# Seven-product weight chunks: one weight sum made by an adding transfer, and the sums and products in another order

## The chip, the cores and the metric

One Trainium2 chip; the kernel runs on one of its cores. The metric is the device time of one execution in microseconds (us). The engines are TensorE (PE in the profile; its weight loads are PEld), VectorE (DVE), ScalarE (ACT), GpSimd (POOL) and SyncE (SP, which here only starts transfers).

## The reference, cut to what matters

A model of two layers on 256 tokens of width 1024, all in fp32. Each layer has a first feed-forward block, a token mixer, a cross attention and a second feed-forward block, each followed by a layer norm:

```python
def swiglu(x, w_gate, w_up, w_down):
    return (jax.nn.silu(x @ w_gate) * (x @ w_up)) @ w_down

for l in range(2):
    h = layer_norm(ALPHA * h + 0.5 * swiglu(h, ffn1_gate[l], ffn1_up[l], ffn1_down[l]), ln_g[l, 0], ln_b[l, 0])
    ...
    h = layer_norm(ALPHA * h + 0.5 * swiglu(h, ffn2_gate[l], ffn2_up[l], ffn2_down[l]), ln_g[l, 3], ln_b[l, 3])
```

The gate and up weights are 1024 x 2816, the down weight is 2816 x 1024. There are four such blocks in all; the change is in them alone.

## The kernel before, in words

**Products.** An fp32 product is made of three matmuls. Every 128 x 1024 piece of a weight is loaded to a `raw` tile; ACT copies it, rounded, to a high part `whi`, and DVE subtracts that from the raw values to make the low part `wlo` (`split`, L60; ACT is L61, DVE is L62). The activations have the same two parts (`xTh` and `xTl`, `ah` and `al`). `mm_rows` (L129) then issues, for each slice of 128 rows, high x high, high x low and low x high, so the second matmul of every three is the first that reads `wlo`. There are 8 `whi` and 8 `wlo` buffers, given out in turn.

**The feed-forward block** is `ffn` (L400). The 2816 columns are cut into six chunks, five of 512 and one of 256. For a chunk the kernel makes gate and up products, then SiLU(gate) x up (`sg`); four transfers and two transposes on DVE turn that around (`turn`, L446), and it is split into `ah` and `al`. The products with the down weight (`both`, L683, accumulated in the PSUM tiles `dn`) follow one chunk behind: after the hidden products of chunk c come the second half of chunk c-2's down products and the first half of chunk c-1's, each half being one call of `both` with 24 matmuls.

**Chunks of seven products.** The chunks in `sevens` (L666) are computed by a block scheme with seven products of half the size instead of eight: chunks 2 and 4 of each block, and in the first block of layer 0 (the one with `early`) only chunk 4. That makes seven such chunks in all. The tokens, the 1024 rows of the weights and the pair (gate, up) are each halved. `w00` is gate rows 0 to 511, `w10` gate rows 512 to 1023, `w01` up rows 0 to 511, `w11` up rows 512 to 1023, each 512 columns wide and held in two tiles of 128 x 1024. `bx[0]` to `bx[3]` are four combinations of the activations that `blocks_of_x` (L539) makes once for a block. Each product is one call of `run` (L597): four slices of three matmuls, so 12 matmuls, 84 for a chunk.

`by_seven` (L555) issues the loads, then goes through the products in this order, making the parts of each product's weight just ahead of it (`parts_of`, L580; with a second argument it first adds that block into the first, in place, two adds of 128 x 1024 on DVE, L584). PSUM results are combined into `g[0]`, `g[1]`, `e` and `f` by DVE (`put`, L605 and L606) and one ACT copy (L612):

| product | weight | adds of 128 x 1024 ahead of it |
|---|---|---|
| 1 | w00 | none |
| 2 | w00 += w01 | 2 |
| 3 | w00 += w11 | 2 |
| 4 | w01 += w11 | 2 |
| 5 | w11 | none |
| 6 | w10 | none |
| 7 | w00 += w10 | 2 |

The last combinations are in `left` (L628), which runs after `both(c - 2, 1)`.

**What orders the work.** Each engine works through its instructions in one order, set ahead by a scheduler from the program and its buffers. `w00` lies in the tiles `spare0` and `spare1`, `w01` in `lng` and `lnb` (these hold the layer norm's parameters at other times: `ln_params`, L293, loads them for the block's end at chunk 5), `w11` and half of `w10` in the rotating `raw` tiles, the other half of `w10` in `spare2`. All weight loads are issued by SP.

Of the kernel before, what the change touches and what calls it, by code (L numbers as in the profile page):

```python
# [46 lines left out]
def model(ctx: ExitStack, tc: tile.TileContext, t: dict, out: bass.AP):  # L47
# [352 lines left out]
    def ffn(l, name, n, pend=None, last=False, early=None):  # L400
        gate, up, down = (t[f"{name}_{x}"][l] for x in ("gate", "up", "down"))
        with tc.tile_pool(name="ffn", bufs=2, reuse_waits="tile") as fp:
# [40 lines left out]

            def turn(s):  # L446
                ah, al = act_tiles()
                x = fp.tile([P, 4, NT, P], F32, tag="dealt", name="dealt", bufs=1)
                for a in range(4):
                    nc.sync.dma_start(x[a * 32 : a * 32 + 32], s[:, :, a * P : (a + 1) * P])  # L450
                for i in range(NT):
                    d = fp.tile([P, 4, P], F32, tag="up", name="square")
                    nc.vector.transpose(
                        d.rearrange("p k (b r) -> p b k r", b=4), x[:, :, i, :].rearrange("p b (k j) -> p b k j", k=4)
                    )
                    split(ah[:, :, tok(i)], al[:, :, tok(i)], d)
                return ah, al

            def first():
# [62 lines left out]
                        gated(s, i, ou)  # L522
                return turn(s)

            def hidden(c0, between=lambda: None):
                s = activations()
                o = all_products(load(gate, 0, NK, c0, CHUNK))
                for i in range(NT):
                    activate(s, i, o[i])
                between()  # L530
                o = all_products(load(up, 0, NK, c0, CHUNK))
                for i in range(NT):
                    gated(s, i, o[i])
                return turn(s)
# [17 lines left out]
                    split(*parts[n], q[o])  # L552
                return parts

            def by_seven(c0, bx):  # L555
                def rows_by_columns(r):
                    return r.rearrange("p (k c) -> p k c", c=CHUNK)

                def pieces(*tags):
                    return [  # L560
                        rows_by_columns(
                            (fp if "spare" in g else wp).tile([P, DM], F32, tag=g, name="raw", bufs=6 if g == "raw" else 1)
                        )
                        for g in tags
                    ]

                def block(m, j, to):
                    for i in range(2):
                        k = 4 * j + 2 * i
                        loads.append(nc.sync.dma_start(  # L570
                            to[i], m[k * P : (k + 2) * P, c0 : c0 + CHUNK].rearrange("(k p) c -> p k c", p=P)
                        ))
                    return to
# [6 lines left out]
                def parts_of(r, plus=None):  # L580
                    hi, lo = [], []
                    for i in range(2):
                        if plus is not None:
                            nc.vector.tensor_tensor(r[i], r[i], plus[i], op=ALU.add)  # L584
                        h = wp.tile([P, 1024], F32R, tag="whi", name="whi", bufs=8)
                        w = wp.tile([P, 1024], F32R, tag="wlo", name="wlo", bufs=8)
                        h, w = (rows_by_columns(x) for x in (h, w))
                        split(h, w, r[i])
                        hi.append(h)
                        lo.append(w)  # L590
                    return Weights(hi, lo, 2, [])

                def part_of_x(i, j):
                    d = slice(4 * j, 4 * j + 4)
                    return xTh[:, d, tok(i)], xTl[:, d, tok(i)]

                def run(o, x, w):  # L597
                    for k in range(4):
                        wh, wl = w.at(k, slice(0, CHUNK))
                        mm_rows(o, x[0][:, k, :], x[1][:, k, :], wh, wl, k == 0, k == 3)  # L600

                def half_sum():
                    return fp.tile([P, 4, P], F32, tag="up", name="half").rearrange("p k t -> p (k t)")

                def put(o, a, op, b):  # L605
                    nc.vector.tensor_tensor(halves(o), sums(a), halves(b), op=op)  # L606

                s = activations()
                g = [s[:, i, :] for i in range(NT)]
                o = [acc((P, CHUNK)) for _ in range(4)]  # L610
                run(o[0], part_of_x(0, 0), parts_of(w00))
                nc.scalar.copy(halves(g[0]), sums(o[0]))  # L612
# [12 lines left out]
                run(o[2], part_of_x(1, 1), parts_of(w00, w10))  # L625


                def left():  # L628
                    put(e, o[0], ALU.add, e)
                    for i in range(NT):  # L630
                        put(g[i], o[1 + i], ALU.add, g[i])
                    s = fp.tile([P, NT, CHUNK], F32, tag="spare2", name="sg", bufs=1)
                    for i, u in enumerate((e, f)):
# [3 lines left out]
                    return turn(s)  # L637

                return left

# [50 lines left out]
            def aside():  # L691

                with tc.issue_after(lows[-1].ins):
                    if bx:
                        rest[1]()
                    else:
                        bx.extend(blocks_of_x())

            for c, (c0, ncol) in enumerate(chunks):
                if not c:  # L700
                    acts.append(first())
                    ys = [[acc((P, 512), "dn") for _ in range(2)] for _ in range(NT)]
                elif c in sevens:
                    left = by_seven(c0, bx)
                else:
                    if c in (1, 2) and early is not None:
                        acts.append(hidden(c0, aside))
                    else:
                        acts.append(hidden(c0) if ncol == CHUNK else last_hidden(c0))
                if c == 1 and early is None:  # L710
                    bx.extend(blocks_of_x())
                if c == max(sevens) + 1:
                    gb = ln_params(l, n)
                if c == 1 and early is not None:

# [492 lines left out]
```

## Time and profile before

| quantity | value |
|---|---|
| time, median of 3 runs | 1072.19 us (1072.14 to 1073.27) |
| the profiled execution's own time | 1072.23 us |
| its span in the trace | 1070.2 us, so 2.0 us lie outside the span |
| granted TensorE clock, mean | 0.998 |
| busy: PE, DVE, ACT, POOL | 1060.6, 946.3, 642.2, 65.0 us |
| bytes moved by transfers | 231.90 MB |

The profile is of one execution. Busy time is the time in which an engine had an instruction under way. The chain of waits follows the work that ended last back to its start. Windows give the busy time of each engine in a stretch of the span; a row of the timeline joins neighbouring instructions of one kind (x3 is three of them). A line of the table by line that has one line number for a helper (L62, L105) joins all its callers.

### The profile page before, as it was taken

To read this page: it belongs to the slowest core of one execution; us is meant where nothing else is said; L and a number is where in the kernel's file an instruction comes from. 1 tells how busy PE (TensorE), PEld (TensorE's weight loads), DVE (VectorE), ACT (ScalarE), POOL (GpSimd) and SP (SyncE) were. 2 spreads that over 40 slices of the span, in tenths; PEclk is the share of its full clock that TensorE was granted. 3 is DMA by queue.
4 is the path that set the end of the run, shared out by engine and by line. 5 is a ranking of instruction groups with operands and counts; after the bars stand their busy time and mean duration, and the time that the engine had idled before them with its cause. 6 is when DMAs were issued, how large, how long until landed. Compare 5 with 4: busy or idle time off the path is not lost.

```text
span 1070.2 us, 16314 instructions
## 1 busy us (share of the span) xinstructions
PE 1060.6 (99%) x5968; PEld 938.9 (88%) x5968; DVE 946.3 (88%) x1318; ACT 642.2 (60%) x916; POOL 65.0 (6%) x114
## 2 busy tenths in 40 slices
PE   9999999999999999999999999999999999999997
PEld 7888888889899888888888888888898998888886
DVE  6977997998998799999799999788989787999986
ACT  7556655767457565656575557566764665656660
POOL 9600001000000000000000000010000000000000
PEclk9999999999999999999999999999999999999999
DMA  9998395755575575948675875957536665759471
GB/s 360 259 298 269 119 281 167 251 188 159 177 271 168 181 247 198 292 167 226 236 260 192 250 261 173 298 168 227 190 128 208 247 230 176 259 151 341 133 220 40
DMA packets 130896, 231.90 MB, mean 217 GB/s; under 512 B 9409, under 2 KB 48609, under 8 KB 130817
## 3 DMA queue, kind: packets, MB, share of 16 engines
q1 hardware_dynamic: 129024, 228.49, 65.6%
q0 software_dynamic: 1216, 1.20, 0.5%
q8 instruction: 47, 0.77, 0.3%
q10 hardware_dynamic: 576, 1.18, 0.3%
q14 instruction: 33, 0.26, 0.1%
HBM read 216.15 MB, written 1.05 MB: 203 GB/s over the span
## 4 chain that ended last, share of the span: by engine, by line
PE 99%; DMA 0%; DVE 0%; issue 0%; DVEq 0%
PE acc L105 65%; PE dn L105 31%; PE acc L172 1%; PE dn L910 1%; DMA h<-in_x_dram 0%; PE dn L969 0%; PE dn L968 0%; PE dn L958 0%; PE acc L1034 0%; PE dn L472 0%; PE dn L875 0%; DVE h L358 0%; DVE h L353 0%; DVE st L338 0%; DVE h L326 0%
## 5 line engine op out<-in xcount | busy, mean ns | idle before, releaser
L61 ACT CAST whi<-raw 128x1024 fp32r<-128x1024 f32 (+1 forms) x438 | 442.4, 1042 | 199.3 <-DVE raw L584 54.7
L62 DVE TENSOR_TENSOR wlo<-raw,whi 128x1024 fp32r<-128x1024 f32 (+1 forms) x438 | 515.6, 1210 | 33.9 <-ACT whi L61 30.4
L105 PE MATMUL acc<-whi,xT 128*128 128x512 f32 x1032 | 312.9, 380 | 0.0
L105 PEld LDWEIGHTS acc<-whi,xT 128*128 128x128 f32 x1032 | 195.0, 189 | 27.5
L105 PE MATMUL acc<-wlo,xT 128*128 128x512 f32 x516 | 195.6, 379 | 0.0
L105 PE MATMUL acc<-xT,whi 128*128 128x512 f32 x576 | 142.2, 382 | 0.2
L105 PE MATMUL dn<-whi,ah 128*128 128x512 f32 x346 | 131.5, 380 | 0.0
L105 PE MATMUL dn<-wlo,ah 128*128 128x512 f32 x346 | 131.1, 379 | 0.0
L105 PE MATMUL dn<-whi,al 128*128 128x512 f32 x346 | 131.1, 379 | 0.0
L105 PEld LDWEIGHTS acc<-xT,whi 128*128 128x128 f32 x576 | 103.9, 190 | 12.5 <-ACT whi L61 0.7
L105 PEld LDWEIGHTS acc<-wlo,xT 128*128 128x128 f32 x516 | 97.5, 189 | 13.9
L105 PE MATMUL dn<-whi,xT 128*128 128x512 f32 x288 | 87.9, 381 | 0.0
L105 PEld LDWEIGHTS acc<-xT,wlo 128*128 128x128 f32 x576 | 75.5, 191 | 3.9
L105 PE MATMUL acc<-xT,wlo 128*128 128x256 f32 x576 | 75.9, 275 | 0.0
L105 PEld LDWEIGHTS dn<-wlo,ah 128*128 128x128 f32 x346 | 65.4, 189 | 9.2
L105 PEld LDWEIGHTS dn<-whi,al 128*128 128x128 f32 x346 | 65.4, 189 | 9.2
L105 PEld LDWEIGHTS dn<-whi,ah 128*128 128x128 f32 x346 | 65.4, 189 | 9.1
L584 DVE TENSOR_TENSOR raw<-raw 128x1024 f32<-128x1024 f32 x56 | 66.2, 1218 | 0.4
L350 POOL TENSOR_TENSOR rs<-rs,nhalf 128x1 f32<-128x1 f32 x16 | 14.9, 929 | 834.2 <-DVE rs L346 598.7
L105 PEld LDWEIGHTS dn<-whi,xT 128*128 128x128 f32 x288 | 54.6, 190 | 7.4
L105 PE MATMUL dn<-wlo,xT 128*128 128x512 f32 x144 | 54.6, 379 | 0.0
L332 DVE SCALAR_TENSOR_TENSOR h<-h,dn 128x512 f32<-128x512 f32 x31 | 21.2, 683 | 31.6 <-PE dn L105 31.6
(232 smaller groups left out, 1278.7 us busy)
## 6 DMA issues: line engine op xcount, KB each, us to landing
raw<-in_ffn_up_dram SPq DMA_DIRECT2D x88, 512.0 KB, 5.3
raw<-in_ffn_down_dram SPq DMA_DIRECT2D x88, 512.0 KB, 6.9
raw<-in_ffn_gate_dram SPq DMA_DIRECT2D x84, 512.0 KB, 5.0
raw<-in_w_in_dram SPq DMA_DIRECT2D x48, 512.0 KB, 4.7
dealt<-sg SPq DMA_DIRECT2D x80, 128.0 KB, 4.7
raw<-in_ca_k_dram SPq DMA_DIRECT2D x16, 512.0 KB, 5.1
raw<-in_w_out_dram SPq DMA_DIRECT2D x16, 512.0 KB, 4.3
raw<-in_ca_v_dram SPq DMA_DIRECT2D x16, 512.0 KB, 5.3
```

The source lines that it names most:

```text
L61: nc.scalar.copy(hi, src)
L62: lows.append(nc.vector.tensor_tensor(lo, src, hi.bitcast(F32), op=ALU.subtract))
L105: nc.tensor.matmul(o, w, x, start=start, stop=stop)
L172: nc.tensor.transpose(pt[:, k, :], src[:, (4 * j + k) * P : (4 * j + k + 1) * P], unit)
L332: nc.vector.scalar_tensor_tensor(v, v, ALPHA / scale, sums(y[i][n]), op0=ALU.mult, op1=ALU.add, accum_out=None if junk is None else st[:, ...
L350: nc.gpsimd.tensor_tensor(rs, rs, nhalf[:, 0:1], op=ALU.pow)
L584: nc.vector.tensor_tensor(r[i], r[i], plus[i], op=ALU.add)
L910: nc.tensor.matmul(o[g, hh, :], kc[:, hh, g], x, start=True, stop=True)
```

## The change

The seven products are the same as sets of operands; what makes their weights, and the order, are others.

- The sum `w01 + w11` is called `both_up` and is made by transfers: SP loads `w01` into the tiles `lng` and `lnb` as before (L568 after the change), and GpSimd then starts two transfers of 512 KB that add `w11`'s rows into the same tiles (L578, `accum_op=ALU.add`). That is done in `sum_by_transfers`, from `between()` in the chunk before, that is, between its gate and its up products. `w11` is also loaded by itself, as before.
- DVE's adds of 128 x 1024 (L596 after the change) are three pairs instead of four.
- The order of the products, after:

| product | weight | operations of 128 x 1024 ahead of it |
|---|---|---|
| 1 | w00 | none |
| 2 | w11 | none |
| 3 | w10 | none |
| 4 | w00 += both_up | 2 |
| 5 | both_up | none |
| 6 | both_up = w00 - w11, after product 5's split has read both_up | 2 |
| 7 | w00 += w10, after product 6's subtraction has read w00 | 2 |

- The results of products 1 and 2 are copied from PSUM by ACT (two copies instead of one); DVE still combines seven times (L622 after the change).
- The tiles `lng` and `lnb` are now last read by product 6's splits instead of product 4's, so the load of the layer norm's parameters behind chunk 4 waits for those.
- `turn`, `pieces`, `block` and `by_seven` also take a narrower last chunk; `sevens` does not name one, so that code makes no instructions here. The numbers of matmuls are as before.

The core of the diff:

```diff
+            def sum_by_transfers(c0):
+                to = block(up, 0, c0, pieces("lng", "lnb"))
+                for i, r in enumerate(to):
+                    a = (4 + 2 * i) * P
+                    nc.gpsimd.dma_start(
+                        r, up[a : a + 2 * P, c0 : c0 + CHUNK].rearrange("(k p) c -> p k c", p=P), accum_op=ALU.add
+                    )
+                return to
...
-                w00 = block(gate, 0, pieces("spare0", "spare1"))
-                w01 = block(up, 0, pieces("lng", "lnb"))
-                w11 = block(up, 1, pieces("raw", "raw"))
-                w10 = block(gate, 1, pieces("spare2", "raw"))
+                    w00 = block(gate, 0, c0, pieces("spare0", "spare1"))
+                    w11 = block(up, 1, c0, pieces("raw", "raw"))
+                    w10 = block(gate, 1, c0, pieces("spare2", "raw"))
...
                 run(o[0], part_of_x(0, 0), parts_of(w00))
-                nc.scalar.copy(halves(g[0]), sums(o[0]))
-                run(o[2], bx[0], parts_of(w00, w01))
-                run(o[1], bx[1], parts_of(w00, w11))
                 e = half_sum()
-                put(e, o[1], ALU.add, g[0])
-                run(o[3], bx[2], parts_of(w01, w11))
-                put(g[1], o[3], ALU.add, e)
+                nc.scalar.copy(halves(e), sums(o[0]))
+                run(o[1], bx[3], parts_of(w11))
                 f = half_sum()
-                put(f, o[2], ALU.subtract, g[1])
-                put(e, o[2], ALU.subtract, e)
-                o = [acc((P, CHUNK)) for _ in range(3)]
-                run(o[0], bx[3], parts_of(w11))
-                run(o[1], part_of_x(0, 1), parts_of(w10))
-                run(o[2], part_of_x(1, 1), parts_of(w00, w10))
+                nc.scalar.copy(halves(f), sums(o[1]))
+                run(o[2], part_of_x(0, 1), parts_of(w10))
+                combine(g[0], o[2], ALU.add, e)
+                put(w00, w00, ALU.add, both_up)
+                run(o[3], bx[1], parts_of(w00))
+                combine(e, o[3], ALU.add, e)
+                combine(f, f, ALU.subtract, e, apart=False)
+                o = [acc((P, ncol)) for _ in range(3)]
+                run(o[0], bx[2], parts_of(both_up))
+                combine(g[1], o[0], ALU.add, e)
+                put(both_up, w00, ALU.subtract, w11)
+                run(o[1], bx[0], parts_of(both_up))
+                put(w00, w00, ALU.add, w10)
+                run(o[2], part_of_x(1, 1), parts_of(w00))
...
+                if c + 1 in sevens:
+                    n = (c + 1) * CHUNK
+                    if n + CHUNK <= DFF:
+                        both_up[:] = sum_by_transfers(n)
```

The change moves instructions on DVE. Three places are shown, two of them in chunk 2 of the second feed-forward block of layer 0. Before the change the tiles of w00 are raw_4296 and raw_4297, of w01 raw_4300 and raw_4301, of w11 raw_4304 and raw_4305, of w10 raw_4308 and raw_4309. After it, w00 is raw_4303 and raw_4304, both_up raw_4154 and raw_4155, w11 raw_4307 and raw_4308, w10 raw_4311 and raw_4312.

The first place is DVE from the fifth product's first split to the two splits of the seventh. Before, the fifth product is w11's, and the rows are these:

```order
L62 TENSOR_TENSOR wlo_4414<-raw_4304,whi_4413 128x1024
L62 TENSOR_TENSOR wlo_4418<-raw_4305,whi_4417 128x1024
...
L62 TENSOR_TENSOR wlo_4438<-raw_4309,whi_4437 128x1024
L62 TENSOR_TENSOR wlo_4455<-raw_4296,whi_4454 128x1024
L606 TENSOR_TENSOR sg_4312<-acc_4316,half_4382 128x512
L584 TENSOR_TENSOR raw_4297<-raw_4297,raw_4309 128x1024
L606 TENSOR_TENSOR half_4407<-acc_4315,sg_4312 128x512
L606 TENSOR_TENSOR half_4382<-acc_4315,half_4382 128x512
L62 TENSOR_TENSOR wlo_4460<-raw_4297,whi_4459 128x1024
```

After, the fifth product is both_up's:

```order
L62 TENSOR_TENSOR wlo_4413<-raw_4154,whi_4412 128x1024
L596 TENSOR_TENSOR raw_4154<-raw_4303,raw_4307 128x1024
...
L596 TENSOR_TENSOR raw_4155<-raw_4304,raw_4308 128x1024
L622 TENSOR_TENSOR sg_4315<-acc_4318,half_4340 128x512
L62 TENSOR_TENSOR wlo_4436<-raw_4154,whi_4435 128x1024
...
L596 TENSOR_TENSOR raw_4303<-raw_4303,raw_4311 128x1024
L596 TENSOR_TENSOR raw_4304<-raw_4304,raw_4312 128x1024
L622 TENSOR_TENSOR half_4362<-acc_4410,half_4362 128x512
L62 TENSOR_TENSOR wlo_4458<-raw_4303,whi_4457 128x1024
L62 TENSOR_TENSOR wlo_4462<-raw_4304,whi_4461 128x1024
```

From the fifth product's first split to the seventh's second, counting both, DVE has 7 operations of 128 x 1024 and 8 of 128 x 512 before, and 10 and 9 after: one add of 128 x 1024 (L584) stood between them before, four (L596) do so now.

The second place is DVE just ahead of that, at the splits of the earlier products. Before:

```order
L584 TENSOR_TENSOR raw_4297<-raw_4297,raw_4301 128x1024
L584 TENSOR_TENSOR raw_4296<-raw_4296,raw_4304 128x1024
L584 TENSOR_TENSOR raw_4300<-raw_4300,raw_4304 128x1024
L62 TENSOR_TENSOR wlo_4345<-raw_4297,whi_4344 128x1024
...
L584 TENSOR_TENSOR raw_4297<-raw_4297,raw_4305 128x1024
L584 TENSOR_TENSOR raw_4301<-raw_4301,raw_4305 128x1024
L584 TENSOR_TENSOR raw_4296<-raw_4296,raw_4308 128x1024
L62 TENSOR_TENSOR wlo_4367<-raw_4297,whi_4366 128x1024
```

After:

```order
L596 TENSOR_TENSOR raw_4304<-raw_4304,raw_4155 128x1024
L62 TENSOR_TENSOR wlo_4347<-raw_4308,whi_4346 128x1024
L62 TENSOR_TENSOR wlo_4365<-raw_4311,whi_4364 128x1024
...
L62 TENSOR_TENSOR wlo_4388<-raw_4303,whi_4387 128x1024
L62 TENSOR_TENSOR wlo_4392<-raw_4304,whi_4391 128x1024
L62 TENSOR_TENSOR wlo_4413<-raw_4154,whi_4412 128x1024
```

Six of the eight adds stood here and one ahead; now one stands here and one ahead (`raw_4303<-raw_4303,raw_4154`), and DVE comes to the fifth product's split with five fewer adds behind it.

The third place is in chunk 4 of the same block: DVE from the fourth product's first split to the seventh's first. Before, the fourth product's weight is w01 + w11 (raw_4818 and raw_4819), w00 is raw_4814 and raw_4815:

```order
L62 TENSOR_TENSOR wlo_4904<-raw_4818,whi_4903 128x1024
...
L62 TENSOR_TENSOR wlo_4909<-raw_4819,whi_4908 128x1024
L62 TENSOR_TENSOR wlo_4932<-raw_4822,whi_4931 128x1024
L62 TENSOR_TENSOR wlo_4936<-raw_4823,whi_4935 128x1024
L62 TENSOR_TENSOR wlo_4952<-raw_4826,whi_4951 128x1024
L62 TENSOR_TENSOR wlo_4956<-raw_4827,whi_4955 128x1024
L606 TENSOR_TENSOR half_4900<-acc_4832,sg_4830 128x512
L62 TENSOR_TENSOR wlo_4973<-raw_4814,whi_4972 128x1024
```

After, the fourth product's weight is w00 + both_up (raw_4822 and raw_4823), both_up is raw_4651 and raw_4652:

```order
L62 TENSOR_TENSOR wlo_4907<-raw_4822,whi_4906 128x1024
...
L62 TENSOR_TENSOR wlo_4936<-raw_4652,whi_4935 128x1024
L596 TENSOR_TENSOR raw_4651<-raw_4822,raw_4826 128x1024
L596 TENSOR_TENSOR raw_4652<-raw_4823,raw_4827 128x1024
L622 TENSOR_TENSOR sg_4834<-acc_4837,half_4859 128x512
L62 TENSOR_TENSOR wlo_4955<-raw_4651,whi_4954 128x1024
...
L596 TENSOR_TENSOR raw_4823<-raw_4823,raw_4831 128x1024
L622 TENSOR_TENSOR sg_4834<-acc_4928,half_4859 128x512
L62 TENSOR_TENSOR wlo_4977<-raw_4822,whi_4976 128x1024
```

From the one split to the other, counting both, there were 7 operations of 128 x 1024 and 3 of 128 x 512 (two of these are a transposed chunk's low parts); there are 11 and 6 now, four adds (L596) and three combinations more.

More of the change, by code (lines that the diff above doesn't have):

```diff
@@ L523, in first, with hidden @@
                 return turn(s)
-            def hidden(c0, between=lambda: None):
+            def hidden(c0, between):
                 s = activations()
@@ new lines, in by_seven, with put, parts_of @@
+            def by_seven(c0, bx, both_up=None):
+                ncol = min(CHUNK, DFF - c0)
+                if both_up is not None:
+                    w00 = block(gate, 0, c0, pieces("spare0", "spare1"))
+                    w11 = block(up, 1, c0, pieces("raw", "raw"))
+                    w10 = block(gate, 1, c0, pieces("spare2", "raw"))
+                else:
+                    w00, both_up, w11, w10 = (
+                        block(m, j, c0, pieces("raw", width=ncol)) for m, j in ((gate, 0), (up, 0), (up, 1), (gate, 1))
+                    )
+                def put(o, a, op, b):
+                    for x, y, z in zip(o, a, b):
+                        nc.vector.tensor_tensor(x, y, z, op=op)
+                def parts_of(r):
@@ L608, in by_seven, with combine @@
+                def combine(o, a, op, b, apart=True):
+                    nc.vector.tensor_tensor(halves(o), sums(a) if apart else halves(a), halves(b), op=op)
                 s = activations()
-                g = [s[:, i, :] for i in range(NT)]
-                o = [acc((P, CHUNK)) for _ in range(4)]
+                g = [s[:, i, 0:ncol] for i in range(NT)]
+                if ncol < CHUNK:
+                    put(both_up, both_up, ALU.add, w11)
+                o = [acc((P, ncol)) for _ in range(4)]
@@ L703, in ffn @@
                 elif c in sevens:
-                    left = by_seven(c0, bx)
+                    left = by_seven(c0, bx, both_up if ncol == CHUNK else None)
                 else:
[L706 to L709, printed above, removed]
+                    acts.append(hidden(c0, between) if ncol == CHUNK else last_hidden(c0))
                 if c == 1 and early is None:
                     bx.extend(blocks_of_x())
-                if c == max(sevens) + 1:
+                if c == len(chunks) - 1:
                     gb = ln_params(l, n)
```

87 lines of the change are left out of this document (41 added, 46 removed).

## Prediction

> **What bounds the kernel now.** I read the page first, then the chain of waits, windows over one block's chunks, and the timeline around a chunk of seven products. The page's busy times:
>
> ```profile
> PE 1060.6 (99%) x5968; PEld 938.9 (88%) x5968; DVE 946.3 (88%) x1318; ACT 642.2 (60%) x916; POOL 65.0 (6%) x114
> ```
>
> PE is busy for 1060.6 of 1070.2 us: all that can be gained without fewer matmuls is 9.6 us, and that lies at the ends. The windows (columns: length, then busy time and instructions of PE, PEld, DVE, ACT, POOL, then clock, DMA share, GB/s) show the first 20 us, the stretch ahead of a seven-product chunk 2, that chunk, the same for chunk 4, and the end:
>
> ```profile
> 0.00:20.00 20.00, 17.92 (x76) 14.97 (x77) 13.30 (x18) 13.46 (x19) 19.16 (x41) 1.00 0.92 349
> 396.00:417.00 21.00, 21.00 (x99) 18.39 (x98) 19.95 (x24) 10.65 (x15) 0.00 (x0) 1.00 0.60 207
> 417.00:435.10 18.10, 18.10 (x85) 15.81 (x84) 18.10 (x21) 11.73 (x14) 0.00 (x0) 1.00 0.67 187
> 476.60:494.70 18.10, 18.10 (x85) 15.87 (x84) 18.10 (x21) 14.84 (x16) 0.00 (x0) 1.00 0.55 175
> 1060.00:1080.00 20.00, 2.87 (x26) 2.67 (x24) 5.74 (x14) 0.00 (x0) 0.92 (x1) 0.85 0.13 48
> ```
>
> Inside the chunks PE has no gap, and DVE has none either: it supplies the parts just in time. The chain of waits is PE from end to end (start, length):
>
> ```profile
> 412.00 5.18 PE dn L105 x24
> 417.18 18.13 PE acc L105 x84
> 435.31 10.36 PE dn L105 x48
> ```
>
> So a chunk of seven takes PE 18.13 us, 2.59 us a product, 0.216 us a matmul. PE's own matmuls start at 417.02 (the chain counts 0.16 us later), the fifth product at 427.38, the seventh at 432.56. The question is only whether DVE still delivers each low part by then.
>
> **The adds that go.** The group by line and shape on DVE (busy us, mean ns):
>
> ```profile
> L584 DVE TENSOR_TENSOR raw<-raw 128x1024 f32<-128x1024 f32 x56 | 66.2, 1218 | 0.4
> ```
>
> Two adds fewer in each of seven chunks: 14 x 1.218 = 17.1 us less DVE work. On the path that sets the end it is worth nothing, since PE waits for DVE nowhere in these stages. A rule speaks otherwise: the Trainium skill, Perfetto Trace Analysis, section Identifying the Most-Contended Engine, says to optimize first the engine with the highest occupancy, and to judge TensorE by its weight loads' busy share and not by its matmuls'. By that rule weight loads and DVE stand level (88% each on the page), and DVE's 17.1 us could count in full; the trace disagrees for this kernel, since 84 matmuls fill 18.10 of 18.10 us. I take zero; the most that a gain could be is bounded by the idle 9.6 us, which the change does not touch.
>
> **The adds that move.** DVE's timeline around chunk 2 (start, length, count):
>
> ```profile
> 402.58 1.18 DVE L584 TENSOR_TENSOR raw<-raw 128x1024 f32<-128x1024 f32 x1
> ...
> 407.15 3.49 DVE L584 TENSOR_TENSOR raw<-raw 128x1024 f32<-128x1024 f32 x3
> ...
> 411.69 0.75 DVE L440 TENSOR_TENSOR sg<-acc,sg 128x256 f32<-128x256 f32 x2
> ...
> 417.56 5.76 DVE L62 TENSOR_TENSOR wlo<-raw,whi 128x1024 fp32r<-128x1024 f32 x5
> 423.23 1.30 DVE L453 STREAM_TRANSPOSE square<-dealt 128x512 f32<-128x512 f32 x2
> ...
> 425.56 1.28 DVE L62 TENSOR_TENSOR al<-square,ah 128x512 fp32r<-128x512 f32 x2
> ...
> 432.64 3.50 DVE L62 TENSOR_TENSOR wlo<-raw,whi 128x1024 fp32r<-128x1024 f32 x3
> ```
>
> Back to back, an operation of 128 x 1024 costs (3.49 - 1.22) / 2 = 1.135 us from start to start, one of 128 x 512 about 0.60. The first of the three at 432.64 is the seventh product's second low part; it ends at 433.86, and PE reads it here:
>
> ```profile
> 434.07 0.38 PE L105 MATMUL acc<-wlo,xT 128*128 128x512 f32 x1
> ```
>
> The lead is 0.2 us. That is all the room at the seventh product of a chunk 2.
>
> What DVE cannot do early is set by the eight high-part buffers, that is, four products. The fifth product's first high part takes the buffer of the first product's first half, which PE leaves after six matmuls. PE's and ACT's rows:
>
> ```profile
> 418.10 0.59 PE L105 MATMUL acc<-whi,xT 128*128 128x512 f32 x2
> ```
> ```profile
> 415.48 4.13 ACT L61 CAST whi<-raw 128x1024 fp32r<-128x1024 f32 x4 [4.82 <-DVE raw L584]
> 419.85 1.06 ACT L61 CAST whi<-raw 128x1024 fp32r<-128x1024 f32 x1 [0.24 <-PE acc L105]
> ```
>
> The sixth matmul starts at 418.10 and ends at 418.48; the last of the four casts is the fifth product's, and ends at 419.61 (the next one waits for PE in the same way). This gate stays where it is. What changes is the work behind it. Before, one add stood between the fifth product's first split and the seventh's second; now four do, because product 6's weight overwrites both_up after product 5's split has read it, and product 7's overwrites w00 after that. DVE comes earlier to the gate: the two adds left ahead of it are those at 402.58 and 407.15, then come two splits to 410.6, the products of chunk 1 (the second pair when PE turns to dn at 412.00, so to about 412.9) and three splits to 416.3, or later as ACT's casts allow. It then waits for the cast until 419.63, 1.3 us earlier than the 417.56 + 3 x 1.135 = 420.96 at which the same split starts now.
>
> From 419.63, up to the seventh product's first split, DVE has 8 operations of 1.135 (9.08) and 9 of 0.60 (5.44): that split starts at 434.15 and ends at 435.37. PE's second matmul of the product, the first that reads it, is due at 432.56 + 0.22 = 432.78; with 0.08 us for the hand-over it goes at 435.45. **The seventh product of chunk 2 waits 2.67 us**: about 1.0 for the high part (the add ends at 432.5, the cast takes 1.05, to 433.6 instead of 432.56), the rest for the low part. The second half's split ends 1.135 later, and PE needs it 1.30 after the first half's, so nothing is added. There are three such chunks (the first block of layer 0 has only chunk 4): 3 x 2.67 = 8.0 us.
>
> In chunk 4 the gate lies one product earlier, and PE starts 59.57 us after chunk 2 (476.75 against 417.18), so its seventh product is due at 492.13:
>
> ```profile
> 475.55 1.05 ACT L61 CAST whi<-raw 128x1024 fp32r<-128x1024 f32 x1 [2.59 <-PE dn L105]
> ```
>
> That is the fourth product's first half, in both orders; it ends at 476.60. Behind it, up to the seventh product's first split, stand 10 operations of 1.135 and 6 of 0.60: 14.95, so that split starts at about 491.6 and ends at 492.8, against 492.35 at PE. The stall is about 0.5 us; four chunks, 2.0 us.
>
> The unknown is small waits or leads of DVE for a PSUM result within the stretch. I bound each stall by one DVE operation either way (1.1, taken as 1.0): chunk 2 from 1.7 to 3.7, chunk 4 from 0 to 1.5.
>
> **The adding transfers.** The trace shows no adding transfer. The nearest rows (KB each, us from issue to landing), and SP's load of the tile, which starts when the layer norm has let go of it:
>
> ```profile
> raw<-in_ffn_up_dram SPq DMA_DIRECT2D x88, 512.0 KB, 5.3
> ...
> m<-in_mem_dram POOLq DMA_DIRECT2D x32, 32.0 KB, 6.0
> ```
> ```profile
> 375.85 0.37 SPq L570 DMA_DIRECT2D raw<-in_ffn_up_dram  x1
> ...
> 378.77 0.46 SPq L570 DMA_DIRECT2D raw<-in_ffn_up_dram  x1
> ```
>
> The plain load lands by about 381 to 384, GpSimd then starts the adding one, and DVE wants the first tile at 402.58 and the second at 407.15: 21 us of room. Between the plain 5.3 and four times that, 21.2, the adding transfer costs nothing; I take 8, nearest to the rows, and no cost. The 7 MB more are read in stages where transfers take 0.60 to 0.67 of the engines. GpSimd itself has nothing waited for behind them there: it is 6% busy. If DVE's cover were gone it would stand with every split behind it; that is a rival below.
>
> **The rest.** ACT makes one copy more in each chunk, and it lies within the 40% of the time that ACT is idle:
>
> ```profile
> L612 ACT COPY sg<-acc 128x512 f32<-128x512 f32 x7 | 4.1, 580 | 0.0
> ```
>
> The layer norm's parameters behind chunk 4 are issued after product 6's splits, some 8 us later than these rows:
>
> ```profile
> 479.82 0.33 SPq L296 DMA_DIRECT2D lng<-in_ln_g_dram  x1
> 482.20 0.33 SPq L297 DMA_DIRECT2D lnb<-in_ln_b_dram  x1
> ...
> 484.43 2.65 SPq L77 DMA_DIRECT2D raw<-in_ffn_gate_dram  x2
> ```
>
> Behind them on SP stands a gate load of chunk 5 that PE reads only after the down products, at 505.24 by the chain; issued at 488 and landing 5.3 later, as the up loads do, it is split by 496. It costs nothing; without the 9 us left it would cost what it is late.
>
> **Rivals.**
> *DVE has room after all (no change, 1072.2).* The mechanism: 2.4 us of adds are gone from each chunk and DVE reaches the gate 1.3 us earlier. It decides if the seventh product's first split of chunk 2 is done by 432.78 instead of 435.45, that is, if 2.7 us of the 15.7 behind the gate were not there: three operations done ahead of the gate would do it. For it: DVE stands still for 3.3 us ahead of the gate. Against it: the order is fixed, and the four adds need product 5's split. It is the rival on the other side.
> *The adding transfer is late (about 1099).* At 30 us from its issue (five times the 6.0 row) it lands at 411.5, 8.9 after 402.58; DVE's 3.3 us of standing take up part, 5.6 x 3 = 17 is left on top: 1082.2 + 17 = 1099. It decides beyond about 24 us. For it: no row shows such a transfer. Against: both nearest rows are a quarter of that.
> *The clock falls with the stalls (about 1088).* The last window, mostly idle, has a clock of 0.85. If the 10.36 us of down products behind each stall in chunk 2 ran so, that is 10.36 / 0.85 - 10.36 = 1.8, three times 5.5. Against: the first window has 2.1 us of idle PE and a clock of 1.00. The Trainium skill, TensorE: Matmul & The Clock Gate, section What's actually happening, says that the clock halves after an idle window of some 3.4 us; by that rule stalls of this size cost no clock, and the first window's 1.00 agrees.
> *DVE was the bound (1055).* 1072.2 - 17.1, as the rule on contended engines would have it. Against: PE without a gap.
> That the adds are not removed cannot be: the order shows 42 of them for 56.
>
> **The numbers.** Span 1070.2 + 8.0 + 2.0 = 1080.2; the profiled execution has 2.0 us outside its span (1072.23, the median of the runs is 1072.19): **1082.2 us**. The bounds give 1072.2 + 3 x 1.7 = 1077.3 and 1072.2 + 3 x 3.7 + 4 x 1.5 = 1089.3; with 1.1 us for the scatter of runs (1072.14 to 1073.27) the range is 1076 to 1091. Chances: forecast 0.78, no change 0.09, late transfer 0.06, clock 0.04, DVE as bound 0.03. The range holds the forecast and the clock's case, 0.82. A run can tell about 0.2% (2 us) from no change: faster 0.03, same 0.09, slower 0.88.
>
> **What would show it.** Right: in a chunk 2 PE waits for DVE's low part at the seventh product, by 2.7 us in two pieces, and by about 0.5 in chunk 4, with all other matmuls back to back; DVE idle of some 3 us just ahead of the fifth product's split, waiting for ACT; the group of adds at x42. Wrong: DVE idle at the first adds, waiting for a transfer; a clock under 1.00 behind the stalls; PE without waits at the seventh products; or a wait at another product.

## The result, and the profile after

| | before | after |
|---|---|---|
| median (lowest to highest) | 1072.16 us (1072.04 to 1073.27, 4 runs) | 1085.88 us (1085.21 to 1087.31, 4 runs) |
| span of the profiled execution | 1070.2 us | 1085.5 us |
| that execution's own time | 1072.23 us | 1087.31 us |
| granted clock, mean | 0.998 | 0.995 |

The ratio is 1.0125, with a 95% interval of 1.0109 to 1.0141: the changed kernel is slower by 13.7 us. The forecast was 1082.2, the range 1076 to 1091.

The page's busy times after the change:

```profile
PE 1065.8 (98%) x5968; PEld 939.6 (87%) x5968; DVE 933.3 (86%) x1304; ACT 643.7 (59%) x923; POOL 83.3 (8%) x128
```

DVE has lost 13.0 us of work and the kernel has become longer. The list of what PE waited for (us in all, times, longest) has three rows that the kernel before does not have, the first two and the last:

```profile
PE acc L105 <- DVE wlo L62: 5.9, 7, 1.3
PE acc L105 <- ACT whi L61: 3.2, 3, 1.1
...
PE dn L105 <- DVE wlo L62: 0.6, 1, 0.6
```

Seven waits for a low part, one in each chunk of seven products, and three for a high part, one in each chunk 2. DVE's timeline in chunk 2 of the second feed-forward block of layer 0 (start, length, count, and in brackets the idle time before):

```profile
416.94 3.81 DVE L62 TENSOR_TENSOR wlo<-raw,whi 128x1024 fp32r<-128x1024 f32 x3 [2.66 <-ACT whi L61]
420.79 1.22 DVE L596 TENSOR_TENSOR raw<-raw 128x1024 f32<-128x1024 f32 x1
...
431.26 2.35 DVE L596 TENSOR_TENSOR raw<-raw 128x1024 f32<-128x1024 f32 x2
433.53 0.69 DVE L622 TENSOR_TENSOR half<-acc,half 128x512 f32<-128x512 f32 x1
434.13 4.62 DVE L62 TENSOR_TENSOR wlo<-raw,whi 128x1024 fp32r<-128x1024 f32 x4
```

DVE stands still ahead of the gate, waiting for ACT's casts, as it has fewer adds there. ACT in turn waits for PE to leave a high-part buffer (in brackets):

```profile
415.85 1.06 ACT L61 CAST whi<-raw 128x1024 fp32r<-128x1024 f32 x1 [2.83 <-PE dn L105]
...
418.44 1.06 ACT L61 CAST whi<-raw 128x1024 fp32r<-128x1024 f32 x1 [0.24 <-PE acc L105]
```

The cast at 418.44 is the fifth product's first, the gate of the prediction. From there DVE is busy almost without a gap (18.16 of 18.33 us in the first window below), and the first of the four splits at 434.13 is the seventh product's. PE's timeline there:

```profile
432.23 0.38 PE L105 MATMUL acc<-whi,kTl 128*128 128x512 f32 x1
433.67 0.48 PE L105 MATMUL acc<-whi,xT 128*128 128x512 f32 x1 [1.06 <-ACT whi L61]
435.40 0.74 PE L105 MATMUL acc<-wlo,xT 128*128 128x512 f32 x1 [1.25 <-DVE wlo L62]
435.93 1.06 PE L105 MATMUL acc<-whi,xT 128*128 128x512 f32 x2
436.78 0.63 PE L105 MATMUL acc<-wlo,xT 128*128 128x512 f32 x1
...
439.13 0.38 PE L105 MATMUL acc<-wlo,xT 128*128 128x512 f32 x1
```

The sixth product's last matmul starts at 432.23, the next at 433.67, the one that reads the low part at 435.40. Then something comes that the forecast did not count: a pair of matmuls takes 1.06 us where it took 0.59, each starts 0.43 us after the last instead of 0.216, and at 439.13 the old pace is back. Windows over the chunk up to the low part, the 4.2 us behind it and the rest (columns as before, the clock third from the end) show it:

```profile
417.07:435.40 18.33, 16.02 (x73) 13.44 (x72) 18.16 (x21) 10.31 (x13) 1.51 (x2) 1.00 0.43 119
435.40:439.60 4.20, 4.20 (x12) 3.39 (x13) 4.20 (x5) 4.20 (x5) 0.86 (x1) 0.59 0.97 225
439.60:449.90 10.30, 10.30 (x49) 9.04 (x48) 6.78 (x8) 3.09 (x5) 0.00 (x0) 1.00 1.08 332
```

The clock is 1.00, then 0.59 and 1.00 again. So there are two prices in a chunk 2: the wait and, behind it, a stretch at half speed.

The sum over the profiled execution, from starts of matmuls: each chunk 2 loses 432.23 to 433.67 and 433.67 to 435.40 less 0.216 each, and 0.10 more at the next matmul, 2.84 us; three of them 8.5. Each of the three later chunk 4s loses 0.86, the one of the first block 0.61: 3.2. A wait of 0.6 in a chunk 2's down products (at 982.47) loses 0.9. Half speed behind two of the three chunk 2s costs some 1.7 each beside that 0.10: 3.4. Together 16.0; the first long row of products in the chain of waits starts 0.8 earlier in this execution (10.35 against 11.13), so 15.2, for a difference of the spans of 15.3 us. (The list of waits shows less: it counts a wait from the end of the last matmul, 0.38 after its start, where the next would start 0.216 after it.)

### The profile page after: what moved, and what is told of

Same layout as the page of the kernel before. It is cut to its first block, busy times and chain, and to the rows that moved or that the text cites. A ratio compares the mean times of both kernels' runs of the same rounds, so it can differ in the third digit from the quotient of the medians.

```text
span 1085.5 us, 16340 instructions
## 1 busy us (share of the span) xinstructions
PE 1065.8 (98%) x5968; PEld 939.6 (87%) x5968; DVE 933.3 (86%) x1304; ACT 643.7 (59%) x923; POOL 83.3 (8%) x128
## 3 DMA queue, kind: packets, MB, share of 16 engines
HBM read 223.49 MB, written 1.05 MB: 207 GB/s over the span
## 4 chain that ended last, share of the span: by engine, by line
PE 87%; DVE 9%; issue 2%; DMA 1%; ACT 1%; DVEq 0%; ACTq 0%
PE acc L105 55%; PE dn L105 30%; DVE wlo L62 3%; DVE raw L596 3%; PE acc L172 1%; DVE half L622 1%; DMA raw<-in_ffn_gate_dram 1%; DVE sg L622 1%; PE dn L936 1%; DMA h<-in_x_dram 0%; ACT whi L61 0%; DVE al L62 0%; DVE square L453 0%; PE dn L995 0%; PE dn L984 0%
## 5 line engine op out<-in xcount | busy, mean ns | idle before, releaser
L105 PE MATMUL acc<-whi,xT 128*128 128x512 f32 x1032 | 316.4, 382 | 3.2 <-ACT whi L61 3.2
L596 DVE TENSOR_TENSOR raw<-raw 128x1024 f32<-128x1024 f32 x42 | 50.5, 1217 | 0.4
```

What stands on the lines that cost most here:

```text
L105: nc.tensor.matmul(o, w, x, start=start, stop=stop)
L596: nc.vector.tensor_tensor(x, y, z, op=op)
```

## The experiments

**The sums written elsewhere (e_both).** The sixth and the seventh product's weights overwrite tiles whose last split is long done, w11's and w10's, instead of both_up and w00:

```diff
                 put(w00, w00, ALU.add, both_up)
+                put(w11, w00, ALU.subtract, w11)
+                put(w10, w00, ALU.add, w10)
                 run(o[3], bx[1], parts_of(w00))
...
-                put(both_up, w00, ALU.subtract, w11)
-                run(o[1], bx[0], parts_of(both_up))
-                put(w00, w00, ALU.add, w10)
-                run(o[2], part_of_x(1, 1), parts_of(w00))
+                run(o[1], bx[0], parts_of(w11))
+                run(o[2], part_of_x(1, 1), parts_of(w10))
```

> The changed kernel with the sixth product's weight written into w11's tiles (w11 = w00 - w11) and the seventh's into w10's (w10 = w00 + w10), both right after w00 += both_up, so that no add waits for the fifth product's split. Theory (the seventh product waits for the adds behind the gate, and the clock falls behind those waits): all of it goes, no wait of PE for DVE at a seventh product, clock 0.998, 1071 to 1073 us. Rival (the adding transfers and their 7 MB cost the time): stays at 1083 to 1086. Rival that DVE was a bound whose 17 us can be gained: 1060 to 1068.

Measured: 1071.45 us (1071.14 to 1072.02, 11 runs) beside 1072.01 for the kernel before, a ratio of 0.9995 (0.9987 to 1.0004). In PE's timeline no wait is left at the seventh product:

```profile
432.20 0.38 PE L105 MATMUL acc<-whi,kTl 128*128 128x512 f32 x1
432.42 0.38 PE L105 MATMUL acc<-whi,xT 128*128 128x512 f32 x1
432.63 0.38 PE L105 MATMUL acc<-wlo,xT 128*128 128x512 f32 x1
```

This has the adding transfers, the new order of products and six adds, as the changed kernel, and the whole loss is gone. So the loss comes from where the four adds stand. It shows the other side too: 14 adds fewer on DVE buy nothing that the measurement tells from zero.

**The old number of adds (e_dve_sum).** The sum w01 + w11 by DVE ahead of the fourth product, without adding transfers, the other sums as changed:

```diff
-                    nc.gpsimd.dma_start(
-                        r, up[a : a + 2 * P, c0 : c0 + CHUNK].rearrange("(k p) c -> p k c", p=P), accum_op=ALU.add
-                    )
...
+                put(both_up, both_up, ALU.add, w11)
                 put(w00, w00, ALU.add, both_up)
```

> The changed kernel with w01 + w11 made by two adds of DVE ahead of the fourth product again, and no adding transfer; order of products and the other sums as changed. Theory (the place of the adds decides, not their number; DVE stood still 3.9 us ahead of the gate and two adds take 2.3): the same waits at the seventh product, 1084 to 1087 us. Rival (the adding transfers cost): faster than the changed kernel by over 3 us. Rival (DVE's total counts): slower than it by up to 17 us.

Measured: 1086.0 us (1084.13 to 1086.95, 4 runs), 1.0131 (1.0115 to 1.0146), with the same waits in chunk 2 (1.06 and 1.25 us). Here the adding transfers are not what costs the time, and DVE has room for their two adds in what it stands still ahead of the gate.

**One add less behind the gate (e_one_tile).** The second tile of the seventh product's weight goes into w10 early, the first stays late:

```diff
                 put(w00, w00, ALU.add, both_up)
+                put(w10[1:], w00[1:], ALU.add, w10[1:])
...
-                put(w00, w00, ALU.add, w10)
-                run(o[2], part_of_x(1, 1), parts_of(w00))
+                put(w00[:1], w00[:1], ALU.add, w10[:1])
+                run(o[2], part_of_x(1, 1), parts_of([w00[0], w10[1]]))
```

> The changed kernel with one of the seventh product's two adds (its second tile) made into w10 ahead of the gate, so three adds instead of four stand behind it. Theory: the wait at the seventh product shrinks by one operation of 1.14 us: in chunk 2 from 2.84 to about 1.7 us of lost time, in chunk 4 from 0.86 to nothing; if the clock falls only behind pauses of some 2.5 us, no fall is left: 1072.2 + 3 x 1.7 = 1077 us. If it falls behind every pause of over 1.5 us: up to 1082. Rival (transfers): 1083 to 1086.

Measured: 1083.51 us (1081.76 to 1084.61, 4 runs), 1.0107 (1.0094 to 1.0121). That is 6 us more than expected. In chunk 4 no wait is left, as expected. In chunk 2 the waits are 1.05 and 0.77: the high part comes no earlier, as the first tile's add stays where it was, and the low part's split waits for the high part's cast, so a chunk 2 loses 2.36 us and not 1.7 (2.0 of the 6 us). The rest is in chunk 3's first gate products; the chain of waits there (start, length):

```profile
434.94 0.16 issue
435.10 1.23 DVE wlo L62
436.33 0.02 issue
436.35 10.02 DMA raw<-in_ffn_gate_dram
446.37 0.02 issue
446.39 0.04 ACTq L61
446.42 0.04 issue
446.46 1.05 ACT whi L61
447.51 0.54 ACT sg L658
448.05 0.02 issue
448.07 0.04 DVE sg L659
448.11 0.57 issue
448.68 1.23 DVE wlo L62
449.91 0.04 issue
449.95 1.13 PE acc L105 x4
```

The edit lets w10's raw tile be read until the seventh product's second split (435.10 to 436.33). The gate load of chunk 3 waits for that tile, then takes 10.02 us, against a median of 5.7 in this run, beside chunk 4's plain and adding loads; its cast stands ahead of others on ACT, and PE waits 1.50 us for a low part. Both other blocks with a chunk 2 have such a wait, of 1.00 and 0.91; counted from starts the three lose 4.2 us. The edit had moved a buffer's release along with the add. Two more kernels take that apart.

**One add less, without the late tile (e_first_tile).** The first tile's add is made early, not the second's, so the add that stays reads the raw tile early:

```diff
+                put(w10[:1], w00[:1], ALU.add, w10[:1])
...
+                put(w00[1:], w00[1:], ALU.add, w10[1:])
+                run(o[2], part_of_x(1, 1), parts_of([w10[0], w00[1]]))
```

> As e_one_tile, but it is the seventh product's first tile whose add goes into w10 ahead of the gate; the add that stays behind the gate now reads w10's raw tile early, so chunk 3's gate loads get that tile about 3.8 us sooner than in e_one_tile, with the same number of adds behind the gate. Theory (e_one_tile's waits of 0.9 to 1.5 us in chunk 3's first product come from the late tile): those are gone, the seventh product of chunk 2 loses about 1.5 us: 1076 to 1078 us. Rival (another cause in common, such as the transfers' traffic): 1081 to 1084.

Measured: 1075.56 us (1075.39 to 1076.29, 5 runs), 1.0037 (1.0024 to 1.005), 0.4 below the band that was expected. No wait is left in chunk 3 or 4, and one in each chunk 2:

```profile
431.71 0.38 PE L105 MATMUL acc<-whi,xT 128*128 128x512 f32 x1
432.94 0.48 PE L105 MATMUL acc<-wlo,xT 128*128 128x512 f32 x1 [0.85 <-DVE wlo L62]
```

1.23 - 0.22 and 0.10 behind it make 1.1 us for each of three chunks, 3.4, for a measured 3.6. With four adds behind the gate the wait costs 2.84, with three 2.36 or 1.1 (1.1 where the first tile's add is early: the wait is then one piece instead of two, as the high part is early), with none nothing. So it counts which add stays, and not only how many.

**The late tile without the transfers' traffic (e_one_tile_dve).** The kernel of e_one_tile with the sum w01 + w11 by DVE and no adding transfer:

> e_one_tile with w01 + w11 made by DVE and no adding transfer. Theory (the gate loads of chunk 3 start late and then share the DMA engines with chunk 4's plain and adding loads): a gate load takes less than 10 us, the waits in chunk 3 shrink to under 0.5 us, 1076 to 1080 us. Rival (the late start alone decides): 1082 to 1085, as e_one_tile.

Measured: 1080.49 us (1080.12 to 1081.64, 5 runs), 1.0081 (1.0069 to 1.0093), half a microsecond over the band. The waits in chunk 3 are gone, the gate loads' median is 4.9 us and not 5.7; the 1.06 and 0.78 at the seventh product stay, and one stretch at half speed is in the profile. So of these two kernels the late gate load costs PE time only in the one where the adding transfers run beside it, 3.0 us between the medians. (DVE's two adds more are the other difference between them; they were not tried apart.) In the changed kernel the same shows once in the first profile, in the 0.6 us wait of the down products behind a gate load of 8.11 us.

**PE kept at work in the wait (e_filler).** Ten matmuls more between the sixth and the seventh product of chunk 2, into the seventh's PSUM tile before that is started:

```diff
+                for _ in range(10 if c0 == 2 * CHUNK else 0):
+                    product(o[2], xTh[:, 0, tok(0)], kTh[:, 0:2, :].rearrange("p k c -> p (k c)"), True, True)
                 put(w00, w00, ALU.add, w10)
```

> The changed kernel with ten more matmuls of 128 x 512 between the sixth and the seventh product of chunk 2, into the seventh product's own PSUM tile ahead of its start, so the output is the same and PE works 2.2 us of the 2.5 us in which it stood. Theory (the clock falls because PE stands still): no window behind a chunk 2 with a clock under 1.00, and the time falls by what the falls cost, 1.8 us each, two of them in the profiled run: about 1083 us. Rival (half speed behind the wait has another cause): as the changed kernel, 1085 to 1087, or above it by what the matmuls cost.

Measured: 1083.95 us (1083.35 to 1085.82, 4 runs), 1.0116 (1.0102 to 1.013). Its interval overlaps the changed kernel's, so the time alone does not decide. In this profile the waits of three later chunk 4s also differ, 0.35, 0.35 and 1.43 in place of 0.60. The clock is read from the trace. PE works through the wait and goes on at full pace, and the window behind it has a clock of 1.00 in place of 0.59:

```profile
432.39 2.32 PE L105 MATMUL acc<-kTh,xT 128*128 128x512 f32 x10
434.55 0.38 PE L105 MATMUL acc<-whi,xT 128*128 128x512 f32 x1
435.35 0.48 PE L105 MATMUL acc<-wlo,xT 128*128 128x512 f32 x1 [0.42 <-DVE wlo L62]
435.67 0.59 PE L105 MATMUL acc<-whi,xT 128*128 128x512 f32 x2
```
```profile
435.35:439.50 4.15, 4.15 (x19) 3.67 (x20) 4.15 (x5) 4.15 (x5) 1.19 (x1) 1.00 0.94 211
```

**Half speed in further executions (after_second, after_third, filler_second).** Half speed came behind two chunk 2s of three, so one profile of each kernel can be chance. There are two more profiles of the changed kernel and one more of the kernel with added matmuls.

> A second profile of the changed kernel, unaltered. Theory (each half-speed stretch behind the wait of a chunk 2 costs 1.8 us and comes in some executions and not in others): the same waits of PE at the seventh products, and a time of 1083.7 us plus 1.8 for each stretch seen in the trace, up to 0.7 either way (1087.3 with two). Rival (the waits themselves differ from execution to execution): the same number of stretches with another time.

> A third profile of the changed kernel, unaltered; expected as of the second.

> A second profile of the kernel with ten more matmuls ahead of the seventh product of chunk 2, unaltered. Theory (PE that works does not lose its clock): again no half-speed stretch in a chunk 2. Rival (the first profile had none by luck, as two in three executions of a chunk 2 have one): one or more.

Measured: 1085.21, 1087.71 and 1082.72 us. The waits of chunk 2 are the same to 0.01 us in all three profiles of the changed kernel. The second profile has half speed behind one chunk 2, the third behind two, the kernel with added matmuls behind none. Two windows of the second profile, behind the waits of two different chunk 2s, show the two cases side by side:

```profile
435.88:440.00 4.12, 4.12 (x19) 3.64 (x20) 4.12 (x5) 4.12 (x5) 1.03 (x1) 1.00 1.02 235
969.63:973.80 4.17, 4.17 (x12) 3.37 (x13) 4.17 (x5) 4.17 (x5) 1.22 (x1) 0.59 1.02 236
```

19 matmuls in the one, 12 in the other, in nearly the same time. Over three profiles of the changed kernel it came 5 times of 9, with PE at work 0 times of 6. If both kernels had the same rate, all five would fall among the nine about once in 24 (an estimate from these counts), so that PE's standing still is the cause is likely and not beyond doubt. The expected 1083.7 plus 1.8 a stretch gives 1085.5 and 1087.3 for 1085.21 and 1087.71 (in the third one, the wait in the first block's chunk 4 was 1.04 instead of 0.34).

**The transfers alone, in the kernel before (e_before_plus).** Its w01 tiles also take w11 by GpSimd's adding transfers, so the up half of these chunks is computed with another weight; nothing else is changed:

```diff
                 w01 = block(up, 0, pieces("lng", "lnb"))
+                for i in range(2):
+                    k = 4 + 2 * i
+                    nc.gpsimd.dma_start(
+                        w01[i], up[k * P : (k + 2) * P, c0 : c0 + CHUNK].rearrange("(k p) c -> p k c", p=P), accum_op=ALU.add
+                    )
```

> The kernel before with the 14 adding transfers alone: w11 is also added into the tiles of w01 by GpSimd's transfers, so the up half of these chunks is computed with another weight; everything else stands as before. Theory (the transfers have room and cost nothing by themselves): 1071.5 to 1073 us. Rival (their 7 MB and the later landing cost time): 1074 to 1085.

Measured: 1074.55 us, but from 1071.06 to 1079.85 in 12 runs; 1.0029 (1.0016 to 1.0041). The theory was wrong here: they do cost, 2.6 us in the median and from nothing to 8. The profiled execution (1079.85) is the slowest of them. Ahead of its first chunk 2 with seven products (layer 0's second block), ACT waits long for a plain load, of an up weight of chunk 1. The first row is from this kernel; the second is the longest wait of that kind at this place in the kernel before:

```profile
396.87 1.04 ACT L61 CAST whi<-raw 128x1024 fp32r<-128x1024 f32 x1 [4.05 <-DMA raw<-in_ffn_up_dram]
```
```profile
392.21 1.05 ACT L61 CAST whi<-raw 128x1024 fp32r<-128x1024 f32 x1 [0.74 <-DMA raw<-in_ffn_up_dram]
```

SP issues the two up loads of that moment at 386.52 here and at 385.90 in the kernel before, which at that point runs 0.6 us ahead, so they are issued no later; GpSimd starts its adding transfers at 381.99 and 386.80. The other two blocks with a chunk 2 have such waits of 4.53 and 3.87. DVE's splits are late by that, and DVE then has no idle time up to the seventh product, where the kernel before has 0.2 us of lead, and PE waits there (0.67 and 0.78 in the first of three). That the adding transfers slow the load beside them is read from this one profile; it was not tried apart.

**The sums elsewhere, without transfers (e_both_dve_sum).** The first experiment's kernel with w01 + w11 made by DVE: eight adds, none behind the gate.

> e_both with w01 + w11 made by DVE and no adding transfer: eight adds on DVE as in the kernel before, none of them behind the fifth product's split. Theory (PE bounds, and only the place of the adds counts): no wait at a seventh product, 1071 to 1073 us, as e_both, so the adding transfer buys nothing. Rival (DVE has no room for two more adds ahead of the gate in a chunk 2): 1075 or more.

Measured: 1073.06 us (1072.87 to 1073.68, 11 runs), 1.0012 (1.0004 to 1.0021). PE waits 0.3 to 0.6 us in each chunk 2, not at the seventh product but at the fifth, for ACT's copy out of PSUM:

```profile
PE acc L105 <- ACT half L629: 1.2, 3, 0.6
```

The expectation that the adding transfer buys nothing was wrong: with the order right, the adding transfers are worth 1.6 us (1073.06 against 1071.45), and without them this order is 1.1 slower than the kernel before. With the changed kernel and e_dve_sum this makes a square: adds late, 1085.88 with the transfers and 1086.0 without; adds early, 1071.45 and 1073.06. In this square the place of the adds makes 13 to 14 us, the transfers at most 1.6. The best of all kernels tried is the first experiment's, at 1071.45, and its interval does not exclude the kernel before.

## Why the prediction was right, point by point

- *No gain from the removed adds: right.* The first experiment keeps all of them removed and has no waits, and stands at 0.9995. By the Trainium skill's rule (Perfetto Trace Analysis, section Identifying the Most-Contended Engine) DVE's 17 us could have counted; the measurement says that they do not for this kernel. The section names the share of peak work (MFU) beside the weight loads' share; the prediction used only the second. The page shows 14.8 us less work on DVE in e_both (946.3 to 931.5). In e_both's own order the adds removed are worth 1.6 us, through a wait for ACT that the forecast did not have; against the kernel before they are worth nothing that can be measured.
- *The gate and the sum behind it: right.* The seventh product's first split was to start at 434.15 and starts at 434.13; PE's second matmul was to go at 435.45 and goes at 435.40. These times can be compared as they stand, since PE starts the chunk at 416.90 after the change and at 417.02 before; that is luck, as the 0.6 us lost in the first block's chunk 4 and the 0.8 us earlier start of the execution nearly cancel. DVE's standing still was there, but not just ahead of the fifth product's split: 2.66 us ahead of the fourth product's splits and 1.08 ahead of that, each time for a cast of ACT that waits for PE.
- *Each wait's size: slightly low.* 2.67 was forecast for a chunk 2. Counted in the same way, from the starts of matmuls, it is 2.74, and the next matmul starts 0.10 late as well: 2.84. In chunk 4 about 0.5 was forecast and 0.76 + 0.10 is lost: from the gate to the seventh product's split DVE takes 15.2 us (481.03 to 496.25) where 14.95 was taken, and 0.16 of that is a wait for ACT, a small wait of the kind that the prediction named as its unknown. Together 11.7 us measured for 10.0.
- *The clock: wrongly excluded.* It was a rival at 0.04, instead of the wait's own cost behind it, and "a clock under 1.00 behind the stalls" was named as a sign of being wrong; that sign came. The argument was that the first window has 2.1 us of idle PE and a clock of 1.00; but that idle time is a piece of 1.53 and one of 0.55, with 2.5 us of matmuls between them. Half speed came behind 5 of 9 waits of chunk 2 and cost some 1.7 us each, 2.8 us an execution in the mean; 11.7 and 2.8 are 14.5, for 13.7 measured, and the starts of two executions differ by up to 0.8. The rival's 1.8 us for each stall was close by luck: it took a clock of 0.85 over 10.36 us, and the trace has some 8 matmuls at half speed. The Trainium skill, TensorE: Matmul & The Clock Gate, section What's actually happening, says that the clock halves after an idle window of some 3.4 us, and that these windows run freely. The traces agree with the second, since equal waits had it and had it not; with the first, taken as a wholly idle window, they do not: PE stood still for 1.06 and 1.25 us around one matmul, not for 3.4.
- *The adding transfers: right here, but with a condition that was left out.* They landed in 8.3 us in the median (8 was taken), and DVE's adds waited 0.4 us in all. The room for their own landing was there. What the forecast left out is that plain loads beside them can land later, as in the profile of e_before_plus. Here DVE had idle time ahead of the gate to take that up (e_dve_sum costs the same); in the kernel before, which has 0.2 us of lead, the transfers cost 2.6 us, and beside late gate loads some 3. That the idle time is what made the difference is argued from these runs and was not tried by itself.
- *The rivals:* DVE having room (1072) and DVE as bound (1055) fell, and so did the late transfer (1099). The clock's case was not a rival but a part of the truth.
- *The layer norm's parameters and ACT's copy: nothing of them shows.* No wait of PE in the changed kernel's profile names them. Without the adding transfers and with the sums early, ACT's copy does show (e_both_dve_sum).

The chance of slower, 0.88, came from the right mechanism. The 3.7 us between 1082.2 and 1085.88 are 1.7 of wait and the clock for the rest; the clock's mean of 2.8 would make it 4.5, and the 0.8 between them is open. That 1085.88 lies in the range is in part luck: its upper end, 1091, was worked out from longer waits of DVE alone, and the clock's case, about 1088, happened to lie below it.

## What to carry to other kernels

Count what stands behind a gate, not what an engine has to do in all: here 14 operations fewer made the kernel slower by 13.7 us, because three more adds stood between the moment a buffer came free and the moment PE needed the result. When a sum is made in place, look for a tile whose last reader is already done; that edit alone took the loss away here. And when a forecast has a wait on the engine that bounds the kernel, price what comes behind the wait too: the clock, and the loads that got their tile late.

## What the runs showed of the hardware that had not been expected

- Half speed after short pauses: pauses of 1.06 and 1.25 us with one matmul between them were followed by some 8 matmuls at 0.43 us each (clock 0.59 over 4.2 us) 5 times of 9 in the changed kernel, and 2 times of 3 in the profile with DVE's sums (e_dve_sum); pauses of 1.05 and 0.77 us once in 6 (e_one_tile and e_one_tile_dve); single pauses of 0.85 us never in 3 (e_first_tile). With ten matmuls in the first pause and 0.42 us of the second left it came never in 6.
- In the changed kernel an adding transfer of 512 KB from GpSimd takes 5.8 to 10.6 us from issue to landing, 8.3 in the median, where a plain load of an up weight by SP takes 5.8 in the median; GpSimd is busy for 1.2 us to start one:

```profile
raw<-in_ffn_up_dram SPq DMA_DIRECT2D x88, 512.0 KB, 5.8
...
raw<-in_ffn_up_dram POOLq DMA_DIRECT2D x14, 512.0 KB, 8.3
```
